# Attention averages with the high and low parts of v side by side as 128 stationary columns, and two query tiles moving together

## The chip, the core and the metric

The kernel runs on one core of a Trainium2 chip. The metric is the device time of one execution in microseconds (us); smaller is better. A core has a matrix engine (TensorE, PE below), VectorE (DVE), ScalarE (ACT), GpSimd (POOL) and SyncE (SP, which here issues transfers). Each has its own list of instructions and they meet at semaphores.

## What is computed

A two-layer encoder trunk for 512 frames of width 1024. Each layer has a mixer (latent attention beside a convolution, one output projection), an attention to 256 memory tokens, and a feed-forward part, each with its residual and a layer norm. The change lies in the mixer's attention, cut here to what matters:

```python
SEQ, D_MODEL, DEPTH, CHUNK, Q_BLOCK = 512, 1024, 2, 64, 128
MLA_HEADS, V_HEAD_DIM = 8, 64

for start in range(0, S, Q_BLOCK):
    end = start + Q_BLOCK
    s = (jnp.einsum('bqhd,bkhd->bhqk', q_nope[:, start:end], k_nope[:, :end])
         + jnp.einsum('bqhr,bkr->bhqk', q_rope[:, start:end], k_rope[:, :end]))
    mask = k_chunk[None, :] <= q_chunk[:, None]
    s = jnp.where(mask[None, None], s.astype(jnp.float32) * scale, -jnp.inf)
    p = jax.nn.softmax(s, axis=-1).astype(v.dtype)
    outs.append(jnp.einsum('bhqk,bkhd->bqhd', p, v[:, :end]))
...
# the conv group: GLU, causal depthwise convolution of 31 taps, layer norm, silu
# mixer: concatenate([y_att, y_conv]) @ w_o
```

Query tile t (0 to 3, 128 rows each) sees the key blocks 0 to t. The averages are the last einsum.

## The kernel before

Everything is float32, made of two reduced-precision parts: a number is hi + lo, and a product of two such numbers is three matmuls, hi x hi, hi x lo and lo x hi. `mm3` (L248) issues these three, so lines L250, L251 and L252 appear in every group of matmuls; tiles called whi and wlo are the two parts of a weight, kt, qTh and qTl those of keys and queries, ph and pl those of the transposed probabilities, vv both of v, ya and yc those of the attention's and the convolution's outputs. `split_steps` makes the parts: a cast on ACT (L238, or L240 with a scale) and a subtraction on DVE (L243, L245).

One mixer is one plan. Each piece of work is a generator that yields steps (engine, planned cost, slots that it takes and gives back, events that it waits for). `Weave` holds a clock for each engine, and picks, again and again, the step that can start first by these clocks, the lower rank first among steps that start together. The order in which it emits instructions is the order in which each engine runs them. Slots are counted: ps (banks for scores and transposes), acc and fill and cv (accumulator banks), big (tiles of 128x1024), raw and ring (weights as loaded, weights split), scr (scratch).

The streams of one mixer that the text speaks of:

- `keys(pair)` (L758), `queries(pair, t)` (L780) and `values(t)` (L815) make kt, qTh, qTl and vv; four pairs of heads. vv is one tile of 128 x 512 each for hi and lo, the heads' 64 columns side by side.
- `item_steps` (L835 to L885) is the attention in items. Of a pair there are six: query tile 0 with both heads, tile 1 with both heads, tile 2 with each head, tile 3 with each head. An item has the scores on PE; a reduction to the row maximum on DVE (L847); the exponentials on ACT (L852); a reciprocal and the scaling on DVE (L855, L858); transposes of p on PE (L863); the split to ph and pl; and the averages on PE. An average takes the 64 columns of a head's vv as the stationary side and 128 columns of ph or pl as the moving one, three matmuls for each block, into 64 partitions of a bank. When a head's tile 3 is through, its bank is split to ya.
- `conv_out(t)` (L906 to L940) normalises the convolution's block t: transposes (L911), statistics and scaling on DVE, transposes back (L925), eight ACT operations (four Tanh, L930, and four Identity, L932), a product on DVE (L935) and the split to yc.
- `memory_kv` (L536 to L583) makes keys and values of the memory for the next part, in chunks of 24 matmuls 256 wide between mTh, mTl and the weights. For every two chunks there is one accumulator bank, which an ACT copy to st (L568, L582) empties.
- `output_half(t)` (L952) is the first half of the output projection, which starts with what is ready of ya and yc. The second half follows behind the mixer's plan.

Behind each weight's load stand a cast whi on ACT (L225, L287, L314) and a subtraction wlo on POOL or DVE (L322, L226).

The lines that one average is made of:

```python
for i, par in enumerate(hs):
    for b in range(t + 1):
        mm3(outs[pair][par][0:64, blk(t)], cut(vt[b], ALL, blk(2 * pair + par, VD)),
            (ph[:, blk(i * (t + 1) + b)], pl[:, blk(i * (t + 1) + b)]), b == 0, b == t)
```

## Time and profile before

| what | value |
|---|---|
| median of 3 runs | 1489.97 us (1489.95 to 1490.55) |
| profiled execution | 1493.32 us |
| span of the profile, first to last instruction | 1491.4 us |
| PE busy | 1453.1 us, 97% |
| DVE, ACT, POOL busy | 707.6 (47%), 721.8 (48%), 466.8 (31%) us |
| chain of work that ended last | PE 75%, DVE 12%, ACT 5%, DMA 4%, POOL 3% |
| granted TensorE clock, mean | 0.994 of full speed |

Busy is the time in which an engine has an instruction in flight. Matmuls overlap in the array, so what one costs in a row of its kind is the distance between the starts of two neighbours and not the duration that the profile gives. The two mixers lie at about 60 to 240 us and 790 to 980 us of the span.

### The profile page before, as it was taken

To read this page: it belongs to the slowest core of one execution; us is meant where nothing else is said; L and a number is where in the kernel's file an instruction comes from. 1 tells how busy PE (TensorE), PEld (TensorE's weight loads), DVE (VectorE), ACT (ScalarE), POOL (GpSimd) and SP (SyncE) were. 2 spreads that over 40 slices of the span, in tenths; PEclk is the share of its full clock that TensorE was granted. 3 is DMA by queue.
4 is the path that set the end of the run, shared out by engine and by line. 5 is a ranking of instruction groups with operands and counts; after the bars stand their busy time and mean duration, and the time that the engine had idled before them with its cause. 6 is when DMAs were issued, how large, how long until landed. Compare 5 with 4: busy or idle time off the path is not lost.

```text
span 1491.4 us, 21169 instructions
## 1 busy us (share of the span) xinstructions
PE 1453.1 (97%) x8152; PEld 1256.3 (84%) x8152; DVE 707.6 (47%) x1187; ACT 721.8 (48%) x1278; POOL 466.8 (31%) x665
## 2 busy tenths in 40 slices
PE   8799999999999999999999999999999999999997
PEld 7699988987988888888889999888889888888886
DVE  6999677665511111220469886685663111114005
ACT  3667773453544444553146777624525444446430
POOL 2679771000311111111148877410012111111111
PEclk9899999999999999999999999999999999999999
DMA  5325444242598888998433444423419888889871
GB/s 179 127 70 171 114 128 156 78 161 73 141 223 193 193 196 192 221 201 193 118 116 122 130 127 127 156 71 100 156 48 236 196 190 194 194 193 219 196 140 57
DMA packets 64452, 227.27 MB, mean 152 GB/s; under 512 B 7328, under 2 KB 7360, under 8 KB 64352
## 3 DMA queue, kind: packets, MB, share of 16 engines
q1 hardware_dynamic: 43616, 150.75, 31.1%
q0 software_dynamic: 20736, 75.17, 27.8%
q8 instruction: 64, 1.05, 0.3%
q14 instruction: 36, 0.29, 0.1%
HBM read 213.31 MB, written 8.39 MB: 149 GB/s over the span
## 4 chain that ended last, share of the span: by engine, by line
PE 75%; DVE 12%; ACT 5%; DMA 4%; POOL 3%; issue 1%; SPq 0%; POOLq 0%; DVEq 0%; ACTq 0%
PE accb L250 18%; PE accb L251 18%; PE accb L252 18%; PE psb L250 5%; PE psb L251 5%; PE psb L252 5%; DVE convb L628 3%; DMA raw<-in_xo 3%; DVE wlo L226 1%; DVE p L858 1%; DMA raw<-in_xq 1%; ACT whi L225 1%; PE convb L250 1%; PE convb L252 1%; PE convb L251 1%
## 5 line engine op out<-in xcount | busy, mean ns | idle before, releaser
L250 PE MATMUL accb<-xTh,whi 128*128 128x512 f32 (+1 forms) x1104 | 400.6, 365 | 1.5 <-ACT whi L225 1.3
L251 PE MATMUL accb<-xTl,whi 128*128 128x512 f32 (+1 forms) x1104 | 401.0, 364 | 0.5 <-DVE xTl L432 0.5
L252 PE MATMUL accb<-xTh,wlo 128*128 128x512 f32 (+1 forms) x1104 | 400.3, 363 | 0.1
L287 ACT CAST whi<-raw 128x1024 fp32r<-128x1024 f32 x126 | 132.7, 1055 | 339.4 <-PE accb L251 255.6
L250 PEld LDWEIGHTS accb<-xTh,whi 128*128 128x128 f32 x1104 | 208.7, 190 | 35.7 <-ACT xTh L429 2.7
L251 PEld LDWEIGHTS accb<-xTl,whi 128*128 128x128 f32 x1104 | 209.9, 190 | 32.9 <-DVE xTl L432 1.7
L252 PEld LDWEIGHTS accb<-xTh,wlo 128*128 128x128 f32 x1104 | 209.7, 190 | 32.5 <-DVE wlo L226 0.4
L289 POOL DMA_DIRECT2D wlo<-in_fin x82 | 71.0, 866 | 345.9 <-ACT wlo L288 336.6
L322 POOL TENSOR_TENSOR wlo<-raw,whi 128x1024 fp32r<-128x1024 f32 (+1 forms) x63 | 152.3, 2420 | 62.1 <-ACT whi L314 61.9
L1098 DVE SCALAR_TENSOR_TENSOR scr<-scr,accb 128x512 f32<-128x512 f32 x44 | 30.3, 688 | 253.4 <-ACT scr L1097 253.4
L628 DVE SCALAR_TENSOR_TENSOR convb<-ch,hvec,convb 128x511 f32<-128x511 f32 (+9 forms) x180 | 132.3, 735 | 5.2 <-ACT convb L625 1.7
L288 ACT ACTIVATE wlo<-whi 128x1024 fp32r<-128x1024 f32 x126 | 133.2, 1057 | 2.2
L226 DVE TENSOR_TENSOR wlo<-raw,whi 128x1024 fp32r<-128x1024 f32 (+1 forms) x49 | 56.5, 1158 | 127.2 <-ACT whi L225 126.4
L446 POOL TENSOR_SCALAR ve<-mv 128x1 f32<-128x1 f32 x32 | 27.5, 859 | 244.5 <-DVE mv L467 235.4
L289 POOL DMA_DIRECT2D wlo<-in_fdn x44 | 38.0, 863 | 198.4 <-ACT wlo L288 193.1
L1100 DVE SCALAR_TENSOR_TENSOR hid<-scr,accb 128x512 f32<-128x512 f32 x44 | 30.2, 687 | 136.7 <-PE accb L252 136.7
L225 ACT CAST whi<-raw 128x1024 fp32r<-128x1024 f32 (+1 forms) x49 | 48.9, 1002 | 84.9 <-PE accb L252 33.3
L619 POOL TENSOR_TENSOR cs<-cs,scr 128x511 f32<-128x511 f32 (+29 forms) x60 | 71.5, 1191 | 35.7 <-ACT scr L617 34.5
L314 ACT CAST whi<-raw 128x1024 fp32r<-128x1024 f32 (+1 forms) x63 | 66.7, 1060 | 4.6 <-PE accb L252 1.7
L250 PE MATMUL accb<-whi,hs 128*128 128x512 f32 x176 | 68.6, 390 | 0.0
L251 PE MATMUL accb<-wlo,hs 128*128 128x512 f32 x176 | 68.5, 389 | 0.0
L252 PE MATMUL accb<-whi,hs 128*128 128x512 f32 x176 | 68.5, 389 | 0.0
(295 smaller groups left out, 3165.8 us busy)
## 6 DMA issues: line engine op xcount, KB each, us to landing
raw<-in_fin SPq DMA_DIRECT2D x88, 512.0 KB, 3.6
wlo<-in_fin POOLq DMA_DIRECT2D x82, 512.0 KB, 5.6
raw<-in_fdn SPq DMA_DIRECT2D x44, 512.0 KB, 4.1
wlo<-in_fdn POOLq DMA_DIRECT2D x44, 512.0 KB, 5.9
raw<-in_xk SPq DMA_DIRECT2D x16, 512.0 KB, 3.6
raw<-in_xv SPq DMA_DIRECT2D x16, 512.0 KB, 3.6
raw<-in_wo SPq DMA_DIRECT2D x16, 512.0 KB, 3.6
raw<-in_xq SPq DMA_DIRECT2D x16, 512.0 KB, 3.6
```

Of the source, the lines that this page charges most:

```text
L225: nc.scalar.copy(hi, src)
L226: nc.vector.tensor_tensor(lo, src, hi.bitcast(F32), op=ALU.subtract)
L250: nc.tensor.matmul(o, l[0], r[0], start=first, stop=False)
L251: nc.tensor.matmul(o, l[0], r[1], start=False, stop=False)
L252: nc.tensor.matmul(o, l[1], r[0], start=False, stop=last)
L287: nc.scalar.copy(hi[:, :1024], raw[:, :1024])
L288: nc.scalar.activation(lo[:, :1024], hi[:, :1024].bitcast(F32), AF.Copy, scale=-1.0)
L289: nc.gpsimd.dma_start(out=lo[:, :1024], in_=src, accum_op=ALU.add)
L314: nc.scalar.copy(hi, raw)
L322: eng.tensor_tensor(lo, raw, hi.bitcast(F32), op=ALU.subtract)
L619: nc.gpsimd.tensor_tensor(o[:, d:], o[:, d:], part, op=ALU.add)
L628: nc.vector.scalar_tensor_tensor(out=o[:, d:], in0=src[:, :SEQ - d], scalar=tap(m, d), in1=o[:, d:], op0=ALU.mult, op1=ALU.add)
```

## The change

A head's vv gets the shape (8 heads, 2, 64): hi and lo of one head side by side, 128 columns. One matmul of an average takes all 128 as the stationary side, so one pass of ph makes hi x ph in partitions 0 to 63 of the bank and lo x ph in 64 to 127, and a pass of pl adds hi x pl and lo x pl. An ACT copy (L919) and a DVE addition (L921) bring the two halves together before the split to ya. Two query tiles are moved together, 256 columns, wherever both see the block; `average` does tiles 0 and 1 in 4 matmuls and tiles 2 and 3 in 8. So items are now: tiles 0 and 1 of one head, the same for the other head, tile 2 and tile 3 of the first head, tile 2 and tile 3 of the second. ph and pl of the two late tiles of a head share two big tiles; those of the early ones stay in scratch. The reductions, exponentials and scalings of an early item are done for each tile apart. The product lo x pl, which the kernel before leaves out, is computed too.

The hand-back of the slots that the last keys, queries and values free goes from their own steps to two streams called `released`, and three planned costs are new numbers.

```diff
-            vt[t] = pair_tile("vv")
-            yield from split_steps(o, vt[t][0], vt[t][1], put=("acc",), fire=v_ready[t])
...
-        items = [(pair, t, hs) for pair in range(4)
-                 for t, hs in ((0, (0, 1)), (1, (0, 1)), (2, (0,)), (2, (1,)), (3, (0,)), (3, (1,)))]
+            vt[t] = bigt([P, HEADS, 2, VD], name="vv")
+            yield from split_steps(o.rearrange("p (h c) -> p h c", c=VD), vt[t][:, :, 0, :], vt[t][:, :, 1, :],
+                                   put=("acc",), fire=v_ready[t])
...
+        items = [(pair, ts, par) for pair in range(4)
+                 for ts, par in (((0, 1), 0), ((0, 1), 1), ((2,), 0), ((3,), 0), ((2,), 1), ((3,), 1))]
...
+        def average(o, h, ph, pl, t0):
+
+            n = t0 + 2
+
+            def part(b, p_, start, stop):
+                cols = slice(t0 * P, n * P) if b <= t0 else blk(t0 + 1)
+                mv = p_[:, b] if b <= t0 else p_[:, b, 1]
+                nc.tensor.matmul(o[:, cols], vt[b][:, h].rearrange("p a c -> p (a c)"), mv, start=start, stop=stop)
+
+            part(0, ph, True, False)
+            for b in range(1, n):
+                part(b, ph, False, False)
+                part(b, pl, False, False)
+            part(0, pl, False, True)
...
-            ph, pl = scr(F32R, "ph"), scr(F32R, "pl")
...
+                yield step("PE", 0.46, wait=tuple(v_ready[:2]) + ((mixed[n_item - 1],) if n_item else ()),
+                           get=("acc",), put=("scr", "scr"), fire=mixed[n_item])
+                outs[pair][par] = accb()
+                average(outs[pair][par], h, ph, pl, 0)
...
+            first = ts == (2,)
+            yield pe(nb, P, get=("ps",) + ("big", "big") * first, put=("scr",), wait=() if first else (begun[h],),
+                     fire=begun[h] if first else None)
...
+                late[h] = [bigt([P, 4, 2, P], name=n_) for n_ in ("ph", "pl")]
...
+            yield step("PE", 0.94, wait=tuple(v_ready) + (mixed[n_item - 1],),
+                       get=("scr",) + (("big",) if par == 0 else ()), put=("big", "big"), fire=mixed[n_item])
+            average(outs[pair][par], h, ph, pl, 2)
...
+            yield act(512, fixed=60, wait=(half_done[pair],) if par else ())
+            nc.scalar.copy(y[rows, :], o[other, :])
+            yield dve(512, put=("acc",))
+            nc.vector.tensor_tensor(y[rows, :], o[rows, :], y[rows, :], op=ALU.add)
...
+        def released(n, after):
+            yield step("PE", 0.0, wait=after, put=("big",) * n + ("ring", "ring"))
+
+        wv.add(-1, released(2, (*q_ready[2], *q_ready[3])))
+        wv.add(-1, released(3, (*k_ready[2], *k_ready[3], *v_ready)))
```

The planner makes another order of this in the mixers. Lines behind `average` are about 47 higher: the transposes of p are L887 (early tiles) and L902 (late ones), those of `conv_out` L958 and L972, its Tanh and Identity L977 and L979, the averages L842. Numbers behind a name tell its buffers apart.

PE in layer 0 of the kernel before, between the last two pairs of V chunks of `memory_kv`; the chunk of the second pair begins in the last row:

```order
L863 MATMUL psb_2634<-ident_90,p_2486 128x128 x4
L863 MATMUL psb_2642<-ident_90,p_2557 128x128 x3
L250 MATMUL psb_2650<-kt_2056,qTh_2069 128x384
L251 MATMUL psb_2650<-kt_2056,qTh_2069 128x384
L252 MATMUL psb_2650<-kt_2056,qTl_2070 128x384
L250 MATMUL accb_2656<-whi_840,cTh_961 128x192
L251 MATMUL accb_2656<-wlo_841,cTh_961 128x192
L252 MATMUL accb_2656<-whi_840,cTl_962 128x192
L250 MATMUL accb_2656<-whi_1102,cTh_961 128x192
L251 MATMUL accb_2656<-wlo_1103,cTh_961 128x192
L252 MATMUL accb_2656<-whi_1102,cTl_962 128x192
L250 MATMUL accb_2671<-whi_2519,mTh_638 128x256
```

PE at the same place of the changed kernel; the chunk before ends six rows above the first:

```order
L252 MATMUL accb_2400<-whi_1102,cTl_962 128x192
L972 MATMUL psb_2414<-ident_90,scr_2398 128x128 x4
L972 MATMUL psb_2420<-ident_90,scr_2412 128x128 x4
L958 MATMUL psb_2458<-ident_90,ch_404 128x128
L958 MATMUL psb_2458<-ident_90,cs1_406 128x128
L958 MATMUL psb_2458<-ident_90,ch_405 128x128 x2
L810 MATMUL accb_2400<-ident_90,qs_2407 128x128 x2
L250 MATMUL accb_2485<-whi_2331,mTh_638 128x256
```

Transposes of p, scores and averages stood between the chunks, and now there are queries and the transposes of `conv_out` alone.

ACT in the kernel before, from the last Tanh and Identity of a block of `conv_out` to the copy of st that empties the bank of the chunk before:

```order
L930 ACTIVATE scr_2528<-psb_2523,hvec_400 128x128
L932 ACTIVATE scr_2443<-psb_2523,hvec_400 128x128
L314 CAST whi_2611<-raw_2275 128x1024
L240 ACTIVATE qTh_2069<-accb_2450 128x2x128
L238 CAST yc_2615<-scr_2443 128x512
L582 COPY st_2622<-accb_2531 128x512
L240 ACTIVATE qTh_2493<-accb_2495 128x2x128
```

ACT at the same place of the changed kernel; ahead of the first row stand seven more such pairs, of two blocks:

```order
L977 ACTIVATE scr_2425<-psb_2420,hvec_400 128x128
L979 ACTIVATE scr_2412<-psb_2420,hvec_400 128x128
L314 CAST whi_2469<-raw_2329 128x1024
L240 ACTIVATE qTh_2057<-accb_2400 128x2x128
L582 COPY st_2480<-accb_2334 128x512
```

The copy of st came behind the eight operations of one block, and comes behind the sixteen of two.

PE in layer 1 of the kernel before, at the transposes of the first two blocks of `conv_out`:

```order
L252 MATMUL accb_9357<-cTh_7798,wlo_7606 128x512
L925 MATMUL psb_9369<-ident_90,scr_9355 128x128 x4
L925 MATMUL psb_9379<-ident_90,scr_9366 128x128 x4
L250 MATMUL accb_9387<-whi_7650,cTh_7796 128x192
L251 MATMUL accb_9387<-wlo_7651,cTh_7796 128x192
L252 MATMUL accb_9387<-whi_7650,cTl_7797 128x192
L250 MATMUL accb_9387<-whi_7966,cTh_7796 128x192
L251 MATMUL accb_9387<-wlo_7967,cTh_7796 128x192
L252 MATMUL accb_9387<-whi_7966,cTl_7797 128x192
L863 MATMUL psb_9405<-ident_90,p_9298 128x128 x2
```

PE in layer 1 of the changed kernel, at the same transposes:

```order
L252 MATMUL accb_9149<-whi_9108,mTl_7374 128x256
L972 MATMUL psb_9215<-ident_90,scr_9213 128x128 x4
L958 MATMUL psb_9226<-ident_90,ch_7137 128x128
L958 MATMUL psb_9226<-ident_90,cs1_7139 128x128
L958 MATMUL psb_9226<-ident_90,ch_7138 128x128 x2
L972 MATMUL psb_9231<-ident_90,scr_9224 128x128 x4
L972 MATMUL psb_9273<-ident_90,scr_9266 128x128 x4
L958 MATMUL psb_9279<-ident_90,ch_7137 128x128
L958 MATMUL psb_9279<-ident_90,cs1_7139 128x128
L958 MATMUL psb_9279<-ident_90,ch_7138 128x128 x2
L902 MATMUL psb_9308<-ident_90,p_8972 128x128 x3
```

The third block stood over a hundred rows further on, and now directly follows the second; the queries stand elsewhere.

PE at the end of the attention in layer 0 of the kernel before, the last transposes of p and the last averages (from accb_3012 on):

```order
L863 MATMUL psb_3226<-ident_90,p_3194 128x128 x4
L250 MATMUL convb_3098<-whi_2730,ya_2893 128x512
L251 MATMUL convb_3098<-wlo_2731,ya_2893 128x512
L252 MATMUL convb_3098<-whi_2730,ya_2893 128x512
L250 MATMUL accb_3243<-whi_2667,ya_1941 128x512
L251 MATMUL accb_3243<-wlo_2668,ya_1941 128x512
L252 MATMUL accb_3243<-whi_2667,ya_1941 128x512
L250 MATMUL accb_3243<-whi_2667,ya_2315 128x512
L251 MATMUL accb_3243<-wlo_2668,ya_2315 128x512
L252 MATMUL accb_3243<-whi_2667,ya_2315 128x512
L250 MATMUL accb_3012<-ph_3231,vv_1178 64x128
L251 MATMUL accb_3012<-pl_3232,vv_1178 64x128
```

PE at the end of the attention in layer 0 of the changed kernel, from the last scores to the averages (from accb_3105 on):

```order
L250 MATMUL psb_3115<-kt_2711,qTh_2744 128x512
L251 MATMUL psb_3115<-kt_2711,qTh_2744 128x512
L252 MATMUL psb_3115<-kt_2711,qTl_2745 128x512
L250 MATMUL psb_3119<-kt_2712,qTh_2744 128x384
L251 MATMUL psb_3119<-kt_2712,qTh_2744 128x384
L252 MATMUL psb_3119<-kt_2712,qTl_2745 128x384
L902 MATMUL psb_3139<-ident_90,p_3131 128x128 x4
L902 MATMUL psb_3144<-ident_90,p_3133 128x128 x3
L902 MATMUL psb_3151<-ident_90,p_3037 128x128 x4
L842 MATMUL accb_3105<-ph_2998,vv_1178 128x256
L842 MATMUL accb_3105<-ph_2998,vv_1258 128x256
```

Nine output matmuls stood between the last transposes and the last averages; now the last scores, the transposes and the averages follow one another.

## Rows read from the trace of the kernel before

**Rows 1.** The page's engine table: busy us (share of the span), x instructions.

```profile
PE 1453.1 (97%) x8152; PEld 1256.3 (84%) x8152; DVE 707.6 (47%) x1187; ACT 721.8 (48%) x1278; POOL 466.8 (31%) x665
```

**Rows 2.** Windows: us from start to end, length, busy us of each engine, clock, DMA.

```profile
98.00:174.00 76.00, 73.35 (x609) 69.44 (x608) 64.88 (x121) 58.06 (x145) 66.43 (x105) 1.00 0.50 144
174.00:232.00 58.00, 56.43 (x458) 51.02 (x458) 41.59 (x84) 43.59 (x117) 38.17 (x66) 1.00 0.43 141
826.00:905.00 79.00, 76.30 (x641) 72.27 (x640) 65.47 (x118) 57.64 (x140) 65.37 (x105) 1.00 0.44 133
905.00:973.00 68.00, 64.76 (x481) 57.10 (x481) 44.92 (x90) 46.97 (x128) 39.10 (x68) 0.97 0.44 141
```

**Rows 3.** Tile vv: duration min/median/max of matmuls; idle before them (us, times).

```profile
L250 PE MATMUL accb<-ph,vv x160: 218/223/305, 134.6 to 969.5; 128*64 128x128 f32 x160
...
  DVE pl L243: 8.2, 16
```

**Rows 4.** Timeline of PE, layer 0: start us, duration us, instruction.

```profile
138.88 0.28 PE L252 MATMUL accb<-mTh,wlo 128*128 128x256 f32 x1
139.00 0.22 PE L250 MATMUL accb<-ph,vv 128*64 128x128 f32 x1
139.06 0.23 PE L251 MATMUL accb<-pl,vv 128*64 128x128 f32 x1
...
141.15 0.39 PE L252 MATMUL psb<-kt,qTl 128*128 128x512 f32 x1
141.38 0.40 PE L250 MATMUL psb<-kt,qTh 128*128 128x512 f32 x1
...
147.40 0.27 PE L252 MATMUL psb<-kt,qTl 128*128 128x128 f32 x1
147.51 0.28 PE L250 MATMUL psb<-kt,qTh 128*128 128x128 f32 x1
```

**Rows 5.** Timeline of PE, waits in both layers: in brackets idle before, and its releaser.

```profile
149.61 0.27 PE L251 MATMUL accb<-pl,vv 128*64 128x128 f32 x1 [0.45 <-DVE pl L243]
...
928.24 1.08 PE L863 MATMUL psb<-ident,p 128*128 128x128 f32 x4 [1.03 <-DVE p L858]
```

**Rows 6.** Timeline of ACT, layer 1.

```profile
924.05 0.52 ACT L932 ACTIVATE scr<-psb,hvec 128x128 f32<-128x128 f32 x1
924.39 1.11 ACT L314 CAST whi<-raw 128x1024 fp32r<-128x1024 f32 x1
925.33 0.46 ACT L240 ACTIVATE qTh<-accb 128x256 fp32r<-128x256 f32 x1
925.61 0.55 ACT L852 ACTIVATE p<-psb,mx 128x256 f32<-128x256 f32 x1
```

**Rows 7.** Groups by form, ACT, 95 to 255 us: busy us, mean ns | idle before.

```profile
L238 ACT CAST ph<-psb 128x512 fp32r<-128x512 f32 x12 | 7.1, 589 | 4.5 <-PE psb L863 4.5
...
L852 ACT ACTIVATE p<-psb,mx 128x512 f32<-128x512 f32 x8 | 5.6, 695 | 3.3 <-DVE mx L847 3.3
...
L238 ACT CAST ya<-accb 64x512 fp32r<-64x512 f32 x8 | 4.6, 580 | 3.3 <-PE accb L252 3.1
...
L238 ACT CAST yc<-scr 128x512 fp32r<-128x512 f32 x4 | 2.7, 663 | 0.8 <-DVE scr L935 0.8
...
L582 ACT COPY st<-accb 128x512 f32<-128x512 f32 x4 | 2.5, 617 | 1.3 <-PE accb L252 1.3
```

**Rows 8.** Groups by form, DVE, 95 to 255 us.

```profile
L243 DVE TENSOR_TENSOR pl<-psb,ph 128x512 fp32r<-128x512 f32 x12 | 8.2, 680 | 5.8 <-ACT ph L238 5.8
...
L858 DVE TENSOR_SCALAR p<-p,ri 128x512 f32<-128x512 f32 x8 | 5.4, 678 | 0.3
L243 DVE TENSOR_TENSOR ya<-accb,ya 64x512 fp32r<-64x512 f32 x8 | 5.4, 677 | 1.8 <-ACT ya L238 1.8
L847 DVE TENSOR_REDUCE mx<-psb 128x1 f32<-128x512 f32 x8 | 5.4, 683 | 1.9 <-PE psb L252 1.9
...
L243 DVE TENSOR_TENSOR yc<-scr,yc 128x512 fp32r<-128x512 f32 x4 | 4.3, 1074 | 0.8 <-ACT yc L238 0.7
```

More of the change, by code (lines that the diff above doesn't have):

```diff
@@ L766, in keys @@
                 nc.sync.dma_start(out=tiles[par][oth, :, :].bitcast(F32), in_=kxT_box[0][oth, :, :].bitcast(F32))
-            yield pe(6, SEQ, wait=(wkv[0].ready, wkv[1].ready, *c_ready[1]), get=("acc",),
-                     put=("ring", "ring") if pair == 3 else ())
+            yield pe(6, SEQ, wait=(wkv[0].ready, wkv[1].ready, *c_ready[1]), get=("acc",))
             o = accb()
@@ L783, in queries @@
             yield pe(6, 192, wait=(wq[0].ready, wq[1].ready, c_ready[0][t]) + before,
-                     get=("acc", "scr", "q") + (("big", "big") if t == 0 else ()),
-                     put=("ring", "ring") if pair == 3 and t == 3 else ())
+                     get=("acc", "scr", "q") + (("big", "big") if t == 0 else ()))
             if pair not in qTs:
@@ L838, in item_steps @@
                 before = (mixed[n_item - ITEMS],)
-            yield pe(3 * n, nk, wait=(q_ready[pair][t],) + tuple(k_ready[pair][p_] for p_ in hs) + before,
-                     get=("ps", "scr"))
+            yield step("PE", 3 * sum(max(0.109, w * 0.0004219 + 0.013) for w in width),
+                       wait=tuple(q_ready[pair][t] for t in ts) + (k_ready[pair][par],) + before, get=("ps", "scr"))
             qT = qTs[pair]
             sp = psb()
-            for i, par in enumerate(hs):
-                mm3(sp[:, blk(i, nk)], cut(qT, ALL, par, blk(t)), cut(kts[pair][par], ALL, slice(0, nk)), True, True)
@@ new lines, in item_steps @@
+            for i in range(len(ts)):
+                sl = slice(at[i], at[i] + width[i])
+                nc.vector.tensor_scalar(p[:, sl], p[:, sl], ri[:, i:i + 1], None, op0=ALU.mult)
+            nb = nk // P
+            h = 2 * pair + par
+            if ts == (0, 1):
+                yield pe(nb, P, get=("ps", "scr", "scr"), put=("scr",))
+                pt = psb()
+                for i, src in enumerate((0, 1, None, 2)):
+                    if src is not None:
+                        nc.tensor.transpose(pt[:, blk(i)], p[:, blk(src)], ident)
+                ph, pl = (scr(F32R, n_)[:, :512].rearrange("p (b t c) -> p b t c", t=2, c=P) for n_ in ("ph", "pl"))
+                pv = pt.rearrange("p (b t c) -> p b t c", t=2, c=P)
+                yield from split_steps(pv[:, 0], ph[:, 0], pl[:, 0])
+                yield from split_steps(pv[:, 1, 1], ph[:, 1, 1], pl[:, 1, 1], put=("ps",))
+                yield step("PE", 0.46, wait=tuple(v_ready[:2]) + ((mixed[n_item - 1],) if n_item else ()),
+                           get=("acc",), put=("scr", "scr"), fire=mixed[n_item])
+                outs[pair][par] = accb()
+                average(outs[pair][par], h, ph, pl, 0)
+                return
@@ L863, in item_steps @@
                 nc.tensor.transpose(pt[:, blk(b)], p[:, blk(b)], ident)
-            ph, pl = scr(F32R, "ph"), scr(F32R, "pl")
-            yield from split_steps(pt[:, :nb * P], ph[:, :nb * P], pl[:, :nb * P], put=("ps",))
-            yield pe(3 * nb, P, 64, wait=tuple(v_ready[:t + 1]) + ((mixed[n_item - 1],) if n_item else ()),
-                     get=("acc", "acc") if t == 0 else ("big",) if t == NT - 1 and hs[0] == 0 else (),
-                     put=("scr", "scr"), fire=mixed[n_item])
@@ new lines, in item_steps @@
+            ph, pl = late[h]
+            i = 0 if first else 1
+            yield from split_steps(pt[:, :nk].rearrange("p (b c) -> p b c", c=P), ph[:, 0:nb, i], pl[:, 0:nb, i],
+                                   put=("ps",), fire=mixed[n_item] if first else None)
+            if first:
+                return
+            yield step("PE", 0.94, wait=tuple(v_ready) + (mixed[n_item - 1],),
+                       get=("scr",) + (("big",) if par == 0 else ()), put=("big", "big"), fire=mixed[n_item])
@@ new lines, in item_steps @@
+            average(outs[pair][par], h, ph, pl, 2)
+            if ya[pair] is None:
+                ya[pair] = pair_tile("ya")
+            rows, other = blk(par, 64), blk(1 - par, 64)
+            o, y = outs[pair][par], scr(name="y")[:, :512]
+            yield act(512, fixed=60, wait=(half_done[pair],) if par else ())
+            nc.scalar.copy(y[rows, :], o[other, :])
+            yield dve(512, put=("acc",))
+            nc.vector.tensor_tensor(y[rows, :], o[rows, :], y[rows, :], op=ALU.add)
@@ L883, in mixer @@
+            yield from split_steps(y[rows, :], ya[pair][0][rows, :], ya[pair][1][rows, :],
+                                   put=("scr",) + ("big",) * 4 * par, fire=pair_done[pair] if par else half_done[pair])
         for pair in range(4):
```

55 lines of the change are left out of this document (23 added, 32 removed).

## The prediction

> **What bounds the kernel now.** I read the engine table first: TensorE (PE) is busy for 1453.1 us, 97% of the span [rows 1], so anything that shortens PE's list shortens the kernel and any new PE idle time lengthens it, nearly one for one. The change lies only in the two mixers, so I then read busy time over four stretches, two to a layer [rows 2]: first the one in which the depthwise convolution runs beside the attention, then the one behind it, in which the convolution's blocks are normalised and the attention ends. PE idles 2.65 and 2.70 us in the first kind, and 58.00 - 56.43 = 1.57 and 68.00 - 64.76 = 3.24 in the second; 10.2 us in all. In the second kind VectorE (DVE) and ScalarE (ACT) are at 66 to 75%. So the kernel before keeps PE fed through the mixer with about 5 us lost behind the convolutions. The waits of PE there have one shape [rows 5]: PE stands at a transpose of p or at the second matmul of an average, until DVE has scaled p or made pl. The averages alone cost PE 8.2 us of such waits in 16 places [rows 3], part of it overlapped with matmuls in flight.
>
> **The change part by part.**
>
> *Fewer matmuls for the averages.* Before, a head takes 3 matmuls for each of 1 + 2 + 3 + 4 blocks, 30 of them, 480 over 16 heads of two layers (160 on each of three lines [rows 3]). They are 128 wide on 64 stationary columns and start every 0.060 us (139.00, 139.06 [rows 4]): 28.8 us. After, a head takes 4 matmuls for query tiles 0 and 1 and 8 for tiles 2 and 3; of the 12, eight move 256 columns and four 128, all on 128 stationary columns. On 128 stationary columns a 256-wide matmul takes 0.12 us (138.88 to 139.00) and a 128-wide one 0.11 (147.40 to 147.51) [rows 4]. So a head costs 8 x 0.12 + 4 x 0.11 = 1.40 us, 16 heads 22.4, and PE's list gets 6.4 us shorter. The trace shows both prices on plain matmuls of the same shapes, so I give this term little room: 6.0 to 6.8.
>
> The Trainium skill, "TensorE: Matmul & The Clock Gate", section "Back-to-back issue gap", speaks for a larger gain: it gives some 81 ns for a 128-wide matmul and 131 ns for a 512-wide one in a stream of loads and matmuls, whatever the stationary width. By a line between these, an estimate, the averages would go from 38.9 to 17.7 us, and the whole sum below would be about -0.8 us, no change. Rows 4 disagree with both figures (0.060 us, and 141.15 to 141.38 for a 512-wide one), and the rows decide; I give it one chance in a hundred, inside the middle case.
>
> *More small work for DVE and ACT.* The two halves of the output (high and low v) now lie in different partitions. Each head gets one ACT copy and one DVE addition of 64x512 more; the nearest rows, the cast and subtraction of ya, are 580 and 677 ns [rows 7, 8]. Items are now one head with two tiles (0 and 1), or one head with one late tile, and the splits of the early items come in two pieces. Over 16 heads the copy and the addition alone are 9.3 us of ACT and 10.8 us of DVE. Behind the convolution these engines have a quarter to a third of their time free [rows 2], so by mean load this would cost nothing; what it costs depends on where it stands, which is the next part.
>
> *Another order.* This is the largest part. The late pairs ph, pl now live in two of the big tiles for a head, until both late query tiles are done, and the big slots and weight-ring slots are handed back elsewhere. The planner answers by stopping the attention of layer 0 for lack of big slots until the convolution's blocks and the memory's keys and values are through, and running two and a half head pairs afterwards with little other PE work between. In layer 1 three of the four blocks of the normalised convolution stand in a row. Three places cost.
>
> (1) Layer 0, the last V chunk of the memory. Its bank comes free with the ACT copy of st for the chunk before. In ACT's queue that copy now stands behind the 16 Tanh and Identity of two blocks, one weight cast and one qTh cast, where before it stood behind 8, and PE had averages, transposes and scores ahead of its next chunk. From the end of the chunk PE has six 192-wide matmuls (0.69 us at the 0.115 between 128 and 256 wide), four groups of transposes or their like (8 + 4 + 2 at 0.11: 1.54): 2.23 us of work. ACT can begin its Tanh after 0.69 + 0.44, and then needs 16 x 0.34 (924.05 to 924.39) + 0.94 (924.39 to 925.33) + 0.28 (925.33 to 925.61) [rows 6] + 0.62 for the copy [rows 7] = 7.3. PE waits 1.13 + 7.3 - 2.23 = **6.2 us**. A little later the transposes of both heads' first items of pair 2 stand side by side, and in DVE's queue the scaling of the second p comes behind a reduction, two subtractions of yc (1.07 each), an addition (0.68) and then the scaling itself (up to 0.68) [rows 8]; with 0.68 for the reduction that is 4.2 us, against about 1.1 us of PE work in flight: **3.1 us**.
>
> (2) Layer 1, conv blocks 0 to 2. Their 24 Tanh and Identity and one weight cast are 24 x 0.34 + 0.94 = 9.1 us of ACT, followed by the copy of st (0.62), a cast of yc (0.66) and one of ph (up to 0.59) [rows 6, 7]: 11.0. Before PE gets through the next pair's two first transposes, ACT has a copy, a cast of ph, two of yc, one of ya and another copy ahead of it (0.58 + 0.59 + 1.32 + 0.58 + 0.58) and four short exponentials (at most 0.70 each [rows 7]; I take 0.50), 5.6 us, and DVE a scaling of up to 0.68 behind them [rows 8]: 17.3 us from the first transposes on. PE has 8.9 us of work in that stretch, counted row by row at the prices of rows 4: 34 transposes and their like (3.7), 16 matmuls of two averages (1.9), the scores (1.9) and six output matmuls (1.4). It waits 17.3 - 8.9 = **8.4 us**, in several pieces.
>
> (3) The end of the attention, both layers. The last two scores, eleven transposes and the last averages follow one another with no output projection between. From a score to its transpose stand a reduction (0.68), an exponential (0.70) and a scaling (0.68) [rows 7, 8], 2.1 us, less the 0.5 us of the second scores; the averages then wait for ph and pl (0.59 + 0.68, the subtraction behind another scaling of 0.68) less the 0.3 us of transposes still in flight: 1.6 + 1.6 = **3.2 us** a layer. Before, such waits show as 0.45 to 1.03 us [rows 5], since output matmuls stand between.
>
> *The sum.* -6.4 for the matmuls; -4.8 for the idle time behind the convolutions of before, which the new waits take the place of; +6.2 + 3.1 + 8.4 + 3.2 + 3.2 = +24.1. Together +12.9 us. The profiled execution took 1493.32 us, 1.9 us more than its span of 1491.4, and 3.35 us more than the median of the runs, 1489.97; that is an offset of 0.2% which both kernels will have, so I add the difference to the median: **1503 us**. What bounds the new waits: they can't be below zero, and if ACT and DVE run ahead of PE by more than I allow, half of them may be hidden: +0.9 us. On the other side I left out a dozen smaller waits (0.3 to 1.1 us each, some 9 us), and the 4.8 us may stay: +27. A measurement of this kernel can tell about 0.2%, 3 us, from no change.
>
> **The rivals.** *Faster.* The new waits take no more than the old ones because ACT and DVE are early where I have them late: then only the matmul term is left, 1490.0 - 6.4 = 1483.6 us. For it speaks that neither engine is above 75% behind the convolutions [rows 2]; against it, that ACT's queue can't start a Tanh before PE's transposes, so the 16 and 24 of them can't be done ahead. *Same.* The waits come out at 4 to 9 us more than before, as when only place (1) or only place (2) is real: 1487 to 1493. *The change doesn't do what it says*: a matmul with 128 stationary columns paced by its weight load and not by its 256 columns. Then 0.12 us would grow; rows 4 show the same shape running at 0.12, so no more than 0.14 (128 x 0.02 = 2.6 us back), too little for a case of its own. *Slower by more*: the starved stretch of layer 0 makes the last weights of the next stage late, since ring slots are given back later. A 512 KB weight that comes late costs PE about the cast and subtraction in front of its first matmul, 0.94 [rows 6] and about as much again, a few times; it decides once a load is issued when PE already stands. It belongs to the upper end, 1510 to 1517.
>
> **How the numbers follow.** Starved PE, 1493.2 to 1517 with 1503 the likeliest: 0.68. Faster, 1480 to 1487: 0.20. Within 0.2%: 0.12. Range: 1485 to 1515; about 0.13 lies below and 0.05 above.
>
> **What would show it.** The matmul step: twelve averages a head, at 0.12 and 0.11 us start to start, with no gap from loads. Place (1): one wait of PE over 4 us at a 256-wide matmul of whi and mTh, released by ACT's st. Place (2): PE's busy share below 60% for some 18 us behind the convolution of layer 1, with Tanh and Identity back to back on ACT. Place (3): transposes of p waiting over 1 us for DVE just before the last averages. The four stretches of PE, 10.2 us idle now, should show about 5.4 + 24 = 29, and up to 38 with the small ones. If PE idle there stays near 10, the order did no harm and the time is near 1484. If it is idle for other reasons, a late weight or a slot, the sum was right by chance.

## The result, and the profile after

The changed kernel takes 1532.21 us (median of 4 runs, 1531.13 to 1532.82), the kernel before 1490.26 beside it: a ratio of 1.0273, 95% interval 1.0260 to 1.0286. It is 42 us slower. Forecast were 13, with a range that ended at 25 us slower. The direction was right and PE waits in all three places; the size was not right, and in two of the places the agreement is in part luck.

The page's engine table and the span with its mean clock, after [rows 1]:

```profile
PE 1462.8 (96%) x7864; PEld 1258.0 (82%) x7864; DVE 714.6 (47%) x1235; ACT 736.3 (48%) x1310; POOL 468.4 (31%) x665
```

```profile
core 0: 1530.2 us, clock 0.985
```

PE is busy 9.7 us longer than before though it has 288 matmuls fewer, and idle for 1530.2 - 1462.8 = 67.4 us where it was idle for 1491.4 - 1453.1 = 38.3. Both levels of its clock, 2.4 and 1.2 GHz, are in the mean of 0.985, against 0.994 before. The falls to 1.2 GHz inside the mixers, first the four of the change (start:end, length, busy us of PE, weight loads, DVE, ACT, POOL, granted clock, DMA), then the only one of the kernel before:

```profile
190.10:196.90 6.80, 4.47 (x21) 4.47 (x22) 1.75 (x3) 2.27 (x5) 2.66 (x2) 0.50 0.36 110
210.60:220.80 10.20, 8.21 (x30) 6.95 (x31) 9.64 (x25) 5.61 (x16) 0.24 (x1) 0.50 0.35 103
255.00:258.40 3.40, 3.40 (x18) 3.40 (x18) 1.83 (x4) 1.65 (x3) 0.00 (x0) 0.50 0.99 398
947.90:958.10 10.20, 9.02 (x38) 8.12 (x39) 7.46 (x17) 8.59 (x21) 3.12 (x3) 0.50 0.52 122
```

```profile
928.20:931.60 3.40, 3.36 (x14) 3.39 (x15) 3.26 (x9) 1.53 (x2) 1.36 (x3) 0.50 0.68 230
```

PE is busy for 25.1 us in the four against 3.4 in the one. At half the clock about half of that is lost, an estimate: some 11 us more than before. So the 38.8 us by which the span grew split like this: +29.1 idle, some +11 of work at the lower clock, and about -1 for the rest. That last figure is not the price of the averages, because busy time also holds the last matmul in flight ahead of each wait. From start to start, eight late averages of a head take 0.94 us at full clock and four early ones 0.49 (220.99 to 221.48):

```profile
227.04 0.40 PE L842 MATMUL accb<-ph,vv 128*128 128x256 f32 x2
...
227.98 0.40 PE L250 MATMUL convb<-whi,ya 128*128 128x512 f32 x1
```

That is 1.43 us a head where 30 matmuls at 0.060 took 1.80, or 5.9 us off PE's list (forecast: 6.4).

The same four stretches as rows 2, with both ends moved to where the same work begins and ends in this kernel (same columns):

```profile
98.00:174.00 76.00, 70.77 (x527) 65.97 (x527) 65.61 (x128) 57.99 (x148) 67.75 (x108) 1.00 0.44 131
174.00:258.00 84.00, 68.54 (x409) 59.27 (x408) 43.88 (x97) 51.16 (x133) 39.81 (x64) 0.88 0.32 105
850.00:931.00 81.00, 76.80 (x585) 72.37 (x584) 62.65 (x127) 61.41 (x153) 70.78 (x118) 1.00 0.46 137
931.00:1008.00 77.00, 62.62 (x379) 53.27 (x378) 47.12 (x100) 49.76 (x130) 33.86 (x55) 0.93 0.35 104
```

PE idles 5.2 and 4.2 us beside the convolution, and 15.5 and 14.4 us behind it: 39.3 us against 10.2. All of the added idle time is in these stretches, and in the two behind the convolution the granted clock is 0.88 and 0.93, where rows 2 have 1.00 and 0.97.

The waits of PE there (timeline of PE: start, duration, instruction, in brackets the idle before it and what ended it):

```profile
187.58 0.44 PE L810 MATMUL accb<-ident,qs 128*128 128x128 f32 x2 [1.76 <-POOL qs L807]
192.43 0.58 PE L250 MATMUL accb<-whi,mTh 128*128 128x256 f32 x1 [4.41 <-ACT st L582]
...
254.90 2.52 PE L902 MATMUL psb<-ident,p 128*128 128x128 f32 x11 [1.94 <-DVE ri L875]
...
946.53 0.63 PE L972 MATMUL psb<-ident,scr 128*128 128x128 f32 x4 [3.62 <-DVE scr L968]
...
951.53 1.11 PE L902 MATMUL psb<-ident,p 128*128 128x128 f32 x4 [1.18 <-ACT scr L979]
...
962.71 0.55 PE L887 MATMUL psb<-ident,p 128*128 128x128 f32 x3 [2.25 <-ACT scr L979]
...
976.19 0.33 PE L250 MATMUL accb<-whi,cTh 128*128 128x192 f32 x1 [2.14 <-DVE kt L243]
...
1002.38 1.48 PE L902 MATMUL psb<-ident,p 128*128 128x128 f32 x11 [1.37 <-DVE ri L875]
```

This answers rows 5: waits of 1.2 to 4.4 us where they were 0.45 to 1.03, and no longer only for DVE's scaling of p and pl, but for ACT, POOL and other work of DVE as well. 187.58 and 192.43 are place (1) of the prediction, 946.53 to 962.71 place (2), 254.90 and 1002.38 place (3). The wait of 2.14 us at 976.19 is in none of them. ACT ahead of the wait at 192.43:

```profile
190.14 0.54 ACT L979 ACTIVATE scr<-psb,hvec 128x128 f32<-128x128 f32 x1
190.48 1.13 ACT L314 CAST whi<-raw 128x1024 fp32r<-128x1024 f32 x1
191.41 0.48 ACT L240 ACTIVATE qTh<-accb 128x256 fp32r<-128x256 f32 x1
191.69 0.68 ACT L582 COPY st<-accb 128x512 f32<-128x512 f32 x1
```

The last of sixteen Tanh and Identity begins at 190.14, then come the weight cast, the qTh cast and the copy of st, 0.34, 0.93 and 0.28 us apart as in rows 6; the copy lands and PE goes on. And this is what the prediction did not have, five-microsecond windows over and behind the long waits (same columns as above):

```profile
185.00:190.00 5.00, 1.25 (x10) 0.78 (x8) 1.48 (x3) 5.00 (x15) 2.84 (x9) 1.00 0.31 107
190.00:195.00 5.00, 2.57 (x12) 2.58 (x13) 1.75 (x3) 2.37 (x5) 2.76 (x2) 0.51 0.14 52
210.00:215.00 5.00, 3.32 (x13) 2.75 (x12) 4.72 (x12) 3.49 (x11) 0.17 (x1) 0.56 0.70 209
215.00:220.00 5.00, 4.16 (x14) 3.39 (x15) 4.73 (x13) 2.72 (x9) 0.24 (x1) 0.50 0.00 1
945.00:950.00 5.00, 3.28 (x19) 3.07 (x19) 2.87 (x5) 5.00 (x14) 1.25 (x1) 0.79 0.24 97
950.00:955.00 5.00, 3.82 (x15) 2.92 (x15) 3.19 (x6) 4.95 (x12) 1.86 (x3) 0.50 0.43 94
```

At 185 to 190 PE is busy for 1.25 of 5 us; in the next window the clock is 0.51. From 210 to 220 it is at 1.2 GHz nearly throughout, after a stretch of short waits; and so it is from 950 to 955, behind the wait of 3.62 us. What that does to a matmul is seen in the first V chunk behind the wait, 256 columns, the shape of rows 4:

```profile
193.02 0.41 PE L252 MATMUL accb<-whi,mTl 128*128 128x256 f32 x1
193.23 0.41 PE L250 MATMUL accb<-whi,mTh 128*128 128x256 f32 x1
...
203.41 0.28 PE L842 MATMUL accb<-ph,vv 128*128 128x256 f32 x1
203.53 0.28 PE L842 MATMUL accb<-pl,vv 128*128 128x256 f32 x1
```

It is 0.21 us from start to start, where it is 0.12 at 2.4 GHz (rows 4; and the average's own matmuls at 203.41 and 203.53 keep that pitch).

### The profile page after: what moved, and what is told of

It is laid out like the page before. It is cut to its first block, busy times and chain, and to the rows that moved or that the text cites. A ratio compares the mean times of both kernels' runs of the same rounds, so it can differ in the third digit from the quotient of the medians.

```text
span 1530.2 us, 20684 instructions
## 1 busy us (share of the span) xinstructions
PE 1462.8 (96%) x7864; PEld 1258.0 (82%) x7864; DVE 714.6 (47%) x1235; ACT 736.3 (48%) x1310; POOL 468.4 (31%) x665
## 4 chain that ended last, share of the span: by engine, by line
PE 71%; DVE 14%; ACT 6%; DMA 4%; POOL 3%; issue 2%; DVEq 0%; SPq 0%; POOLq 0%; ACTq 0%
PE accb L250 18%; PE accb L252 17%; PE accb L251 17%; PE psb L252 4%; PE psb L250 4%; PE psb L251 4%; DVE convb L628 3%; DMA raw<-in_xo 3%; DVE wlo L226 1%; DVE p L879 1%; DMA raw<-in_xq 1%; ACT whi L225 1%; POOL wlo L322 1%; PE accb L842 1%; DVE mx L867 1%
## 5 line engine op out<-in xcount | busy, mean ns | idle before, releaser
L250 PEld LDWEIGHTS accb<-xTh,whi 128*128 128x128 f32 x1104 | 208.8, 190 | 35.7 <-ACT xTh L429 2.7
L619 POOL TENSOR_TENSOR cs<-cs,scr 128x511 f32<-128x511 f32 (+29 forms) x60 | 71.7, 1196 | 29.9 <-ACT scr L617 28.7
```

Source lines behind the costliest of these rows:

```text
L250: nc.tensor.matmul(o, l[0], r[0], start=first, stop=False)
L619: nc.gpsimd.tensor_tensor(o[:, d:], o[:, d:], part, op=ALU.add)
```

## The experiments

All were timed beside the kernel before on the same chip; a difference is to that kernel's median in the same set of runs. The last two columns are read from each run's one profiled execution: idle is the span less PE's busy time, and the last is the span times (1 - mean clock). The last counts idle time at the lower clock too, as in a fall at 54 us, ahead of the mixers, and in one behind PE's last matmul: of its 23.0 us for the change some 15 fall on PE's work, and of the 8.9 before some 4.

| run | difference, us | ratio (95%) | PE idle | span x (1 - clock) |
|---|---|---|---|---|
| before | 0 | | 38.3 | 8.9 |
| the change | +42.0 | 1.0273 (1.0260 to 1.0286) | 67.4 | 23.0 |
| e1_release | +17.0 | 1.0112 (1.0096 to 1.0127) | 54.8 | 18.1 |
| e2_before_big24 | +25.7 | 1.0174 (1.0157 to 1.0191) | 53.1 | 16.6 |
| e3_stall | +9.4 | 1.0063 (1.0048 to 1.0079) | 45.3 | 15.0 |
| e4_no_copy_add | +28.7 | 1.0184 (1.0169 to 1.0200) | 62.0 | 19.7 |
| e5_warm | +41.7 | 1.0277 (1.0262 to 1.0292) | 60.1 | 18.4 |
| e6_better_plan | +11.5 | 1.0073 (1.0053 to 1.0092) | 47.2 | 19.5 |
| e7_plan_items4 | +11.1 | 1.0070 (1.0055 to 1.0085) | 48.4 | 16.5 |
| e8_release_no_copy | +6.3 | 1.0032 (1.0021 to 1.0043) | 47.3 | 15.0 |
| e9_before_release | +3.7 | 1.0025 (1.0015 to 1.0034) | 39.6 | 7.5 |
| e10_better_plan_no_copy | +9.7 | 1.0059 (1.0042 to 1.0076) | 48.7 | 18.0 |
| e11_before_twice | +16.6 | 1.0110 (1.0094 to 1.0127) | 48.2 | 10.5 |
| e12_before_costs | +2.9 | 1.0020 (1.0006 to 1.0035) | 39.0 | 10.4 |

Idle and clock together follow the differences in the main; the widest miss is e5_warm, which has 90 transposes more to do.

### Big tiles handed back earlier

```diff
-                       wait=... + before, get=("ps", "scr"))
+                       wait=... + before, get=("ps", "scr"), put=("big",) * 4 * (ts == (3,) and par == 1))
...
-                                   put=("scr",) + ("big",) * 4 * par, fire=...)
+                                   put=("scr",), fire=...)
```

> The changed kernel, but the plan counts the four big tiles of a pair's keys and queries as free right behind that pair's last scores, not behind the split of its output some 8 us later. Theory A (PE stands because the late ph and pl find no big tile, so the attention is put off and other work bunches up): PE's idle time in the mixers falls from 40 us to about 15, the granted clock rises from 0.985 to about 0.993, and the time is 1488 to 1500 us. Theory B (the new averages are themselves costly: 128 stationary columns, one copy and one addition more per head): the waits stay, 1524 to 1532 us.

1509.21 us, 25 us faster than the change. That two edited lines of bookkeeping take back three fifths of the loss, with every instruction of the averages kept, shows that the order, and in it the big tiles, is the larger cause. It did not go as far as expected: the time lies between the two theories, and the idle time fell by 12.6 us and not by 25. One of the long waits stood nearly untouched, in PE's timeline of this run:

```profile
191.37 0.58 PE L250 MATMUL accb<-whi,mTh 128*128 128x256 f32 x1 [3.67 <-ACT st L582]
```

### Fewer big tiles for the kernel before

```diff
-BIG = 26
+BIG = 24
```

> The kernel before, averages and items untouched, with 24 big tiles in place of 26: as many fewer as one head's late ph and pl take. Theory A (a shortage of big tiles): slower by 15 to 40 us, 1505 to 1530, with PE idle and a lower granted clock behind the convolution. Theory B (the cost lies in the new averages): within 6 us of the kernel before, 1487 to 1496.

1517.88 us, 25.7 us slower: theory A, in the kernel without a single one of the new matmuls. So two tiles fewer cost as much as the early hand-back gave. The order is not that of the change, though, and nor are the waits: the longest, one in each layer, are for queries that POOL makes late:

```profile
181.27 0.69 PE L812 MATMUL accb<-ident,qs 128*128 128x128 f32 x2 [3.64 <-POOL qs L809]
...
930.05 0.69 PE L812 MATMUL accb<-ident,qs 128*128 128x128 f32 x2 [4.40 <-POOL qs L809]
```

### The price of one wait

```diff
-            nc.scalar.copy(st, o)
+            for _ in range(10 if h == XH - 2 else 1):
+                nc.scalar.copy(st, o)
```

> The kernel before with one added stall in each layer: for the third head of the memory's values the copy to st is made ten times in place of once (0.62 us each), so that bank comes free 5.6 us later and PE waits for it before a later chunk. This prices a wait of PE by itself. If a wait costs only its own length, the time grows by PE's added idle, about 3 to 5 us a layer, 1496 to 1500 us. If the granted clock falls to 1.2 GHz behind such a wait, the time grows by more than the added idle: some 3 us more for each fall, 1502 to 1512 us, and the windows behind the wait show a granted clock of 0.5 to 0.8.

1501.57 us, 9.4 us slower (7 to 12 by the interval). PE's timeline has the two waits, and the windows over and behind each show the clock:

```profile
197.53 0.41 PE L250 MATMUL accb<-whi,cTh 128*128 128x192 f32 x1 [4.38 <-ACT st L583]
...
928.76 0.58 PE L250 MATMUL accb<-whi,mTh 128*128 128x256 f32 x1 [2.50 <-ACT st L583]
```

```profile
195.00:200.00 5.00, 2.47 (x12) 2.47 (x13) 2.04 (x4) 4.86 (x13) 0.36 (x1) 0.77 0.36 97
200.00:205.00 5.00, 5.00 (x47) 4.91 (x47) 2.08 (x3) 2.01 (x4) 4.92 (x8) 0.89 0.44 164
...
926.00:931.00 5.00, 2.50 (x13) 2.33 (x12) 0.68 (x1) 4.87 (x12) 0.00 (x0) 0.71 0.28 80
931.00:936.00 5.00, 5.00 (x29) 5.00 (x28) 2.43 (x4) 4.95 (x17) 3.03 (x5) 0.60 0.19 77
```

The two waits are 6.9 us, PE's idle time grew by 7.0, and the time by 9.4 (the span of the profiled execution by 11.4): a wait of this size costs about 1.4 times its own length, and by the interval between 1.0 and 1.7 times. PE's order is that of the kernel before, and the granted clock behind the waits is 0.6 to 0.89. One more fall of 3.4 us in this trace, at 344.5, is behind neither of them. The time lies between the two expectations, nearer the second.

### The copy and the addition

```diff
-            nc.scalar.copy(y[rows, :], o[other, :])
...
-            nc.vector.tensor_tensor(y[rows, :], o[rows, :], y[rows, :], op=ALU.add)
-            yield from split_steps(y[rows, :], ya[pair][0][rows, :], ...
+            yield from split_steps(o[rows, :], ya[pair][0][rows, :], ...
```

> The changed kernel without the copy and the addition that bring the two halves of a head's output together (only one half is split to ya, so the other half's contribution is left out of the output); plan and order are the same. Theory A (order and slots): at most 4 us faster, 1527 to 1533 us. Theory B (the added work on ACT and DVE makes the waits): 15 us or more faster, below 1517 us.

1520.83 us, 13 us faster than the change by the two differences, in the same order: neither theory. These two operations for each head, which the prediction put at nothing by mean load, are a third of the loss. With them goes a third effect, which this run does not part from them. In the change the subtraction for ya reads y, a tile in SBUF, where before it read the bank. Timeline of DVE in the change, then of POOL in the same stretch:

```profile
208.77 1.95 DVE L243 TENSOR_TENSOR ya<-y,ya 64x512 fp32r<-64x512 f32 x1
210.65 0.67 DVE L243 TENSOR_TENSOR pl<-psb,ph 128x512 fp32r<-128x512 f32 x1
```

```profile
207.80 2.37 POOL L322 TENSOR_TENSOR wlo<-raw,whi 128x1024 fp32r<-128x1024 f32 x1 [0.49 <-ACT whi L314]
```

and the wait of PE behind it:

```profile
211.37 0.58 PE L842 MATMUL accb<-pl,vv 128*128 128x256 f32 x1 [1.30 <-DVE pl L243]
```

The subtraction of 208.77 takes 1.95 us, beside a subtraction wlo on POOL that lasts from 207.80 to 210.17. Of the 16 in this trace the three that began while such a subtraction, or an addition of the convolution (L619), ran on POOL, and lay beside 0.8 us or more of it, take 1.36, 1.48 and 1.95 us, and the others 0.67 to 0.69; one of these, at 235.63, began just before a wlo on POOL and lay beside 0.65 us of it. Behind the one of 208.77 stands pl, for which PE waits 1.30 us at 211.37. The mean of 1074 ns for yc in rows 8 was such a mixture, too: two single ones of the subtractions for yc in the trace of before take 0.68 and 2.19.

### Keeping PE busy in its waits

```diff
+        def warm(o, n):
+            for _ in range(n):
+                nc.tensor.transpose(o, ident, ident)
...
+            if (l, pair, t) == (0, 2, 3):
+                for _ in range(40):
+                    nc.tensor.transpose(o[:, 256:384], ident, ident)
...
+            warm(pb[:, 0:P], {(0, 3): 10, (1, 2): 30}.get((l, t), 0))
...
+            if (l, pair, par) == (0, 1, 1):
+                warm(outs[pair][par][:, 2 * P:3 * P], 10)
```

> The changed kernel, order untouched, with transposes of the identity put into four of PE's long waits, into columns that later work overwrites: 40 before the q transposes that stand ahead of the last V chunk in layer 0, 10 each before the transposes of conv block 3 and before one average soon after, and 30 before the transposes of conv block 2 in layer 1. They compute nothing that is used. Theory A (behind its waits PE runs at the lower clock, 30.7 us of half clock in the profile, and that is some 14 us of the loss): the waits stay, the clock doesn't fall in these places, 8 to 14 us faster, 1518 to 1524 us. Theory B (the loss is the waits alone; ACT and DVE set the pace behind them anyway): within 4 us of 1532, or slower by the few us of the added transposes.

1532.1 us, no change: the time is that of theory B, but two unlike halves make it. In layer 0 the clock did stay up. The V chunk begins after a wait as before, and runs at 0.12 us:

```profile
191.55 0.28 PE L250 MATMUL accb<-whi,mTh 128*128 128x256 f32 x1
191.67 0.28 PE L251 MATMUL accb<-wlo,mTh 128*128 128x256 f32 x1
...
211.77 0.61 PE L894 MATMUL psb<-ident,p 128*128 128x128 f32 x3 [1.90 <-DVE p L886]
```

(First and second row: the chunk, 0.12 us on. Third: a later wait.) But PE, being early, then waited 1.90 us for DVE where the change waits 0.62 (at 215.25): what the clock gave went into another wait. From the last transposes of conv block 2 to the last q transposes before 224 us this stretch took 36.1 us in place of 38.0; at 1.2 GHz PE worked 3.4 us in it in place of 12.7, so of some 4.6 us that the clock gave back (an estimate, half of the difference) 1.9 came through. In layer 1 the 30 transposes came only when the bank was free, 2 us too late, and were work added: from the first transposes of place (2) to the wait of 2.25 us this run took 23.0 us in place of 21.4. So the clock's 11 us in the split above is what PE spent, not what a steady clock would give back; in layer 0 a part was lost anyway while ACT and DVE were late, and for layer 1 this run doesn't tell.

### Better plans for the new averages

```diff
-BIG = 26
-SCRATCH = 9
+BIG = 25
+SCRATCH = 10
...
-            before = (pair_done[pair - 2],) if pair >= 2 else ()
+            before = (scored[pair - 2],) if pair >= 2 else ()
...
+                       get=("ps", "scr"), put=("big",) * (3 if par else 1) * (ts == (3,)),
+                       fire=scored[pair] if ts == (3,) and par else None)
...
-            yield act(nk, fixed=150 * len(ts), put=("ps",))
+            yield act(nk, fixed=250 * len(ts), put=("ps",))
...
-            yield act(P, 8, put=("ps",))
+            yield act(P, 8, fixed=236, put=("ps",))
```

> The changed kernel's averages with another plan: a pair's big tiles of keys and queries are free behind its last scores, and the next but one pair's keys and queries may start there; 25 big and 10 scratch tiles; and the planned costs of Tanh and Identity, exponentials and reciprocals are those that the trace shows (0.34 us each, 0.1 us more each, 0.19). Theory A (the loss is all order, and PE's list is 6.4 us shorter): PE idle in the mixers at about 10 to 14 us and a clock of 0.993 or more, 1482 to 1490 us. Theory B (the copy and the addition cost PE waits in whatever order): idle 18 us or more, 1494 to 1505.

> As the run with the better plan, but with the planned costs of the changed kernel, 11 scratch tiles, four items in flight in place of three, and a pair's first late item ahead of the second head's early one. Theory A (slots are what starves PE, planned costs matter little): within 5 us of the better plan. Theory B (the planned costs of ACT's small operations, 0.26 us for the 0.34 that the trace shows, are as important as the slots): 10 us or more behind it, with waits of PE for ACT.

1501.84 and 1501.47 us: two plans that differ in costs, slots and items come out alike, 30 us better than the change and 11 above the kernel before. Idle time fell to 47 and 48 us, but some 9 and 8 us more of PE's work than before are still lost to the clock, in four falls of 3 to 7 us each (half of PE's busy time in them, an estimate). The first run's time is that of its theory B, whose reason, the copy and the addition, the last run of the next section doesn't bear out. For the second, theory A holds: right planned costs, which only the first plan has, are worth no more than what else differs (11 scratch tiles, four items, their order); these were not tried apart.

### Both causes taken away, and the copy taken from the better plan

The edits are those of the first and the fourth experiment, and those of the better plan and the fourth.

> The early hand-back of big tiles, and also without the copy and the addition of the two halves (one half is split to ya, the other's contribution is left out of the output). If the two causes add up, 1509 - 11 = 1498 us; if the copy and the addition only cost time where big tiles are short, 1505 to 1510; if they are all that is left besides the matmuls' gain, 1484 to 1490.

> The better plan for the new averages, without the copy and the addition of the two halves (one half is split to ya, the other's contribution is left out of the output). Theory A (what keeps the better plan 11 us above the kernel before is the copy and the addition): 1486 to 1492 us. Theory B (it is order and clock): within 4 us of 1502.

1496.64 and 1499.56 us: in the first the two causes add up, and in the second theory B holds. With early hand-back and without the two operations 35.7 of the 42 us are gone: 25.0 by the first, 10.7 more by the second, nearly additive with the 13.3 by themselves. In the better plan the same two operations cost only 1.8 us, which is not clear of the noise. So their price hangs on the order, and even with both gone and a shorter list the new averages stay 6 us behind. All these runs still have the reductions, exponentials, scalings and splits made in pieces (32 operations more on DVE and 16 on ACT than before, besides the copies and additions) and the two streams `released`; neither was taken out by itself.

### Two more operations for a head in the kernel before

```diff
+                yield act(0, fixed=0)
+                split(outs[pair][par][0:64, :], ya[pair][0][rows, :], ya[pair][1][rows, :])
                 yield from split_steps(outs[pair][par][0:64, :], ya[pair][0][rows, :], ya[pair][1][rows, :],
```

> The kernel before, with the cast and the subtraction of ya made twice for each head (the result is the same): one more ACT and one more DVE operation of 64x512 for a head, as the copy and the addition are, in an order that is otherwise the old one. Theory A (these two operations stand on PE's path whatever the order): 8 to 13 us slower, 1498 to 1503. Theory B (they cost only where PE already waits for the end of a head): within 4 us, 1487 to 1494.

1506.44 us, 16.6 us slower, more than theory A. One cast and one subtraction more for a head, 1.26 us of other engines' time, cost PE 1 us for each of the 16 heads, with PE's order in the mixers as it was. The waits are those of rows 5, longer and more:

```profile
167.45 0.63 PE L863 MATMUL psb<-ident,p 128*128 128x128 f32 x4 [1.88 <-DVE p L858]
...
176.97 0.33 PE L250 MATMUL accb<-whi,cTh 128*128 128x192 f32 x1 [0.75 <-DVE ya L243]
...
180.02 0.52 PE L863 MATMUL psb<-ident,p 128*128 128x128 f32 x2 [1.51 <-DVE p L858]
...
219.44 0.25 PE L250 MATMUL accb<-ph,vv 128*64 128x128 f32 x1 [1.17 <-DVE ya L243]
```

Two wait for the subtraction of ya itself, which holds the slots and banks of the next pair; two for the scaling of p, queued on DVE behind it.

### The kernel before with other plans

The edits of the better plan on the kernel before: first the slots (25 big, 11 scratch, early hand-back), then the planned costs alone.

> The kernel before, its averages untouched, with the early hand-back of a pair's big tiles, the earlier start of the next but one pair, and 25 big and 11 scratch tiles. Is the better use of slots worth something to the old averages too? Theory A (it feeds PE in either kernel): PE idle in the mixers falls from 10 us to 6 to 9, 1484 to 1489 us, faster than both kernels. Theory B (the order of before is already without a shortage): 1489 to 1496.

> The kernel before with planned costs as the trace shows them (Tanh and Identity 0.34 us in place of 0.26, exponentials 0.1 us more, reciprocals 0.19 in place of 0.07). Theory A (right costs make a better order): 1484 to 1488 us. Theory B (a greedy plan's order moves by chance, and this one was picked by time): 1490 to 1502.

3.7 and 2.9 us slower, theory B in both, so the kernel before remains the fastest of those that compute the whole average.

## Why the prediction was wrong in size

The cause that the prediction named for the new order, too few big tiles, is borne out by e1 and e2, at some 25 of the 42 us. What it made of it, term by term:

- **The matmuls.** Right. Averages run at 0.12 us for 256 columns on 128 stationary ones, at 2.4 GHz, and by their starts PE's list is 5.9 us shorter, against the 6.4 that were worked out. The rates that the prediction quoted from the Trainium skill, "TensorE: Matmul & The Clock Gate", section "Back-to-back issue gap", are not what the averages ran at: 0.060 us before and 0.12 after, as rows 4 had it. (By those rates the prediction's sum would come to -1.9 us; its -0.8 is a slip.)
- **Place (1).** The first wait was put at 6.2 us; the trace has 1.76 (for queries that POOL makes) + 4.41 = 6.2, and ACT's queue, which sets the end of both, is as it was worked out. The second was put at 3.1 and came as five shorter ones between 206 and 217 us, 4.2 us together. Only one of the five, 0.62 us, is the forecast one, a transpose of p that waits for DVE's scaling; that the sum comes near is luck.
- **Place (2).** 8.4 us forecast; 946.53 to 965.83 has 3.62 + 0.19 + 1.18 + 2.25 + 0.56 + 0.23 = 8.0. The mechanism, PE behind the Tanh and Identity of several blocks, is there, but the size is in part luck. From the first transposes to the end of the wait at 962.71 it took 21.4 us and not 17.3, and PE was busy for 14.1 of them and not 8.9, mostly at the lower clock. The wait of 2.25 us ends with the Tanh and Identity of the fourth block (959.75 to 962.66), which the forecast did not count. PE's busy share, 14.14 of 21.37, did not fall below the 60% that the prediction named as its sign:

```profile
941.34:962.71 21.37, 14.14 (x73) 12.05 (x72) 13.88 (x30) 18.77 (x51) 6.72 (x7) 0.76 0.39 105
```

- **Place (3).** 3.2 us a layer forecast; 1.94 and 1.37 found, about half. The transposes waited as the first 1.6 us had it; the second 1.6, averages waiting for ph and pl, came to 0.23 us in one layer (1004.41).
- **The sum of idle time.** +24.1 - 4.8 = +19.3 forecast, +29.1 measured. The three places came to 21.7 where 24.1 were forecast, but all other waits of the four stretches to 17.6 where 5.4 had been left. These 12 us are the "dozen smaller waits" that I had left out of the sum and had put at 9, some of them longer than the 1.1 us that I gave them (2.14 at 976.19). They belonged in it: they were counted, and only the range had them.
- **The step that failed: the sum has no term for the clock.** It takes a wait at its own length. Rows 2 have the granted clock of before at 1.00 three times and once at 0.97, over waits of at most a microsecond; that this would not hold over waits six times as long I did not weigh, and no rival did. Some 11 us more of PE's time than before are lost at the lower clock in the trace of the change. Without this term even the upper end (+27) was short of +42.
- **"By mean load this would cost nothing"** was the second step that failed: e4, e8 and e11 put the copy and the addition, or two operations like them, at 11 to 17 us in three orders (and e10 at 2 in a fourth). Half-idle engines on average say nothing on a chain that each head's end goes through. This is another cut of the same 42 us, not an addition to idle time and clock.
- **A reading.** The 8.2 us in 16 places of rows 3 hold the waits of weight loads as well; those of PE's own matmuls are 3.0 us in 7 places. No term of the sum rests on it.
- **The rivals.** "Faster" and "same" fell. "Slower by more" had the wrong mechanism: the longest wait of PE in the mixers for a part of a weight is 0.88 us.

What stays open: how much of the 11 us a steady clock would give back. e3 says that a wait costs some 1.4 times its length (1.0 to 1.7) in an order that is otherwise tight; e5 says that in one stretch where ACT and DVE are late more than half of it comes back as other waits. And why the best plans for the new averages keep losing 8 to 9 us to the clock at idle times only 9 to 10 us above the kernel before was not tried apart.

## What to carry to other kernels

When a change takes more buffers of a shared kind, ask what the planner or the queues will stop doing for lack of them, and count every wait that this makes, the small ones too: here six microseconds of matmuls were bought with two tiles, and the tiles were worth 25. Price a new wait of PE at more than its length wherever PE has so far run without pause (here 1.4 times, by the interval 1.0 to 1.7). A step added at the end of a chain that gives back banks and slots can cost most of its own time, however idle its engine is on average: here 11 to 17 us of some 20 in three orders, and nearly nothing in a fourth.

## What the runs showed of the hardware

The granted clock fell to 1.2 GHz in and behind a wait of 4.41 us (0.51 from 190 to 195 us) and also behind a row of waits of 0.6 to 1.3 us (0.56 and 0.50 from 210 to 220 us); a 256-wide matmul then took 0.21 us in place of 0.12. A DVE subtraction with both sources in SBUF took 0.67 to 0.69 us alone, and 1.95 to 2.2 where it began while a subtraction wlo ran on POOL and lay beside 1.4 us or more of it; with a bank as one source it stayed at 0.68 [rows 8], also beside such a subtraction (0.67 at 207.88 in the kernel before).
